# A hybrid decoder layer: a row's product ahead of a copy, exponentials and copies issued with yields between them, and a last norm with a partial sum as bias

## The chip, the cores and the metric

The kernel runs on one core of a Trainium2 chip. The metric is the device time of one execution in microseconds (us); less is better. A core has five engines that work side by side and wait for each other through semaphores: TensorE (in the profile PE, its weight loads PEld), VectorE (DVE), ScalarE (ACT), GpSimd (POOL) and SyncE (SP). DMA queues move data between the chip's memory and the core's SBUF; here SP issues the weight loads, POOL a few large copies. TensorE writes its results to PSUM, which has eight banks; this kernel uses four as accumulators (`acc`) and four for everything else (`aux`).

## The reference, cut to what matters

One decoder layer over 256 tokens of width 2048, with a norm before and a norm after:

```
h = rms_norm(x, pre_norm_w)
proj = h @ w_in                      # one wide projection, split into q/k/v, gates, b, a ...
A: gated delta rule, 8 heads of 128, in chunks of 64
   qkv = silu(causal_conv(gdn_qkv)); q, k unit norm
   g = cumsum(-exp(a_log) * softplus(a + dt_bias))   per chunk
   decay = exp(g_i - g_j) on and below the diagonal
   L = strict lower part of (beta k) k^T * decay
   T = inverse of (L + I);  u = T (beta v);  states carried from chunk to chunk
   oa = rms_norm(o) * gdn_norm_w * silu(z)
B: causal attention, 8 heads of 128 (256 tokens are one block)
   ob = attention(q, k, v) * silu(z)
merged = sigmoid(gate_a) * (oa @ w_branch_a) + sigmoid(gate_b) * (ob @ w_branch_b)
y = merged @ w_out
out = x + rms_norm(y, post_norm_w)
```

All of it is in float32. `decay` needs the exponentials, the inverse of `L + I` needs the triangles, and the last line needs the mean square of each row of `y`: these are the places that the change touches.

## The kernel before

**Products.** TensorE multiplies in a faster format (`F32R`) to nearly full accuracy: each operand is split into `hi` (a cast, on ScalarE, L213) and `lo` (the rest, on VectorE, L214), and a product is made of hi·hi, hi·lo and lo·hi. Weights are loaded 1 MB at a time through SP into one of three `raw` buffers, and split into one of three `hi`/`lo` buffers. A block of projection is either token-major (`proj_n`, L346: two output tiles of 512 columns, 16 steps of six matmuls each) or head-major (`proj_t`, L328: two heads, 8 steps of eight matmuls).

**What runs beside the products.** Every step ends with a call of `tick` (L131). The other work is written as Python generators in queues: `gq` (decay, scores, inverse, solve of branch A), `vq` (its values), `aq` (two queues of attention heads), `mq`. A generator runs up to its next `yield w` and is then left alone for `w` units; a step takes off half a unit. So a `yield 1` puts two steps of the projection between two pieces of work. Nothing is measured while the kernel runs: the yields only fix the order in which instructions are written. `Queue.drain` (L66) runs what is left of a queue with no steps in between.

**How order becomes execution.** `mm` and `tr` (L138, L141), and some operations of other engines, are wrapped in `pin`, which keeps them in program order. TensorE thus executes exactly in program order. Instructions that are not pinned (casts, the DMA issues on POOL, copies) are ordered by a scheduler at build time, which places an instruction on its engine as early as what it needs allows. An engine executes its own list in order, and waits where an instruction's input is not ready.

**The blocks.** `ORDER` (L39) lists the blocks: `q0 mv0 zg0 q1 kq2 kq3 zg1 v0 v1 v2 ga0 zm0 zm1 ga1 mv1 v3 ga2 ga3 mk0 mk1 gb0 mk2 gb1 mk3 gb2 gb3`. Ahead of them stand a first key projection and the block `zg2`, whose last columns feed the decay. A block `kq` is a key and a query block, `mk` a query and a key block of the attention. After the list come the two branch projections (`ua`, `ub`) and the output projection (`y`).

**What the change and the prediction touch.**

- L314 to L325: after the first norm's factor, `rrow` is copied out of PSUM; `prow` (the convolution's weights as rows) is transposed into the tile `pcp` and copied to `pcol`; then a product of one row, `adrow` (the decay's two parameter rows), with ones spreads it over all partitions into other columns of `pcp`, and it is copied to `nad`.
- `decays` (L375): forms the decay's exponents with VectorE, two heads at a time with `yield 1` between, then four exponentials on ScalarE (L441), each over two heads (128x768), in place in `dec`.
- `scores` (L488), one generator a head: splits keys and queries, multiplies, weighs with `dec`.
- `inverse` (L595): once all heads are scored, writes the triangles to `l_d` in memory, copies all of them to the four partition groups of `lc` (L620, four DMAs on POOL of 512 KB each), waits `L_WAIT` (7 units), and then eliminates column by column on VectorE, 63 columns with a yield after each: 0.6 units, or 2 while `after[0]` is positive, which is so for 16 steps after each value block (`SLOW`, L672). Then the inverse goes through `t_d` to `tt`, and another `L_WAIT`.
- `solve` (L692): products with the inverse (`sv`), then for each of the two token tiles `outputs` (L728): products `so` in two groups of four heads, their squares with sums on ScalarE (L744), a factor `fo` (VectorE, a square root on ScalarE, a reciprocal), products with the gate `os` (L760), a yield of `OS_WAIT` (5), transposes `ot`, and a split into `oaT`.
- `attend` (L802): scores `ms`, softmax, transposes `pp`, products `po`, transposes `pt`; the first head to arrive at L838 asks for `ob_tile()`, a tile that lies where `solve` reads its data (`g0`), so `free_tile` (L677) first drains `gq`.
- `weigh` (L1024) and `finish` (L1034): of each 512 columns of `y`, a square with its sum on ScalarE (into one column of `ssy`) and a product with the norm's weights (`yw`, L1031); after the fourth, the sum of the four columns, a square root, a reciprocal, then scaling with the residual added and the store, for one token tile after the other.

Of the kernel before, what the change touches and what calls it, by code (L numbers as in the profile page):

```python
# [8 lines left out]
F32 = mybir.dt.float32  # L9
F32R = mybir.dt.float32r  # L10
BF16 = mybir.dt.bfloat16
AF = mybir.ActivationFunctionType
ALU = mybir.AluOpType
AX = mybir.AxisListType

P = 128
EPS = 1e-6
# [7 lines left out]
D_WAIT = 7  # L25
SC_WAIT = 4
L_WAIT = 7
INV = (0.6, 2)
SLOW = 8
V_WAIT = 8  # L30
# [41 lines left out]
def hybrid_layer(  # L72
# [15 lines left out]
    nc = tc.nc  # L88
    B, S, D = x.shape
    NT = S // P  # L90
    KT = D // P
    H = a_log.shape[1]
# [45 lines left out]
    def mm(*args, **kwargs):  # L138
        return pin(nc.tensor.matmul(*args, **kwargs))  # L139
# [177 lines left out]
    pcol = cst.tile([P, P], F32, name="pcol")  # L317
    pcp = aux_tile("pcp")
    tr(pcp[:, :P], prow, ident)
    nc.vector.tensor_copy(pcol, pcp[:, :P])  # L320

    mm(pcp[:, P : P + nba], ones[0:1, :], adrow, start=True, stop=True)
    nad = cst.tile([P, nba], F32, name="nad")
    nc.vector.tensor_copy(nad, pcp[:, P : P + nba])
    na, dtb = nad[:, :H], nad[:, H:]  # L325
# [49 lines left out]
    def decays():  # L375

        pbt = [pt[:, ZBA:ZW] for pt in pzg]
        zz = cst.tile([P, NT, H], F32, name="zz")
        sp = cst.tile([P, NT, H], F32, name="sp")
        for t in range(NT):  # L380
            pa_ = pbt[t][:, H:]
            pin(nc.vector.scalar_tensor_tensor(zz[:, t, :], pa_, rstd[:, t : t + 1], dtb, op0=ALU.mult, op1=ALU.add))
        for t in range(NT):
            pb_ = pbt[t][:, :H]
            pin(nc.scalar.activation(beta[:, t, :], pb_, AF.Exp, scale=nrstd[:, t : t + 1]))
        pin(nc.scalar.activation(sp, zz, AF.Abs))
        pin(nc.scalar.activation(sp, sp, AF.Exp, scale=-1.0))
        pin(nc.scalar.activation(na, na, AF.Exp))
        pin(nc.scalar.activation(sp, sp, AF.Ln, bias=ones[:, 0:1]))
        pin(nc.vector.scalar_tensor_tensor(sp, zz, 0.0, sp, op0=ALU.max, op1=ALU.add))  # L390
        pin(
            nc.vector.scalar_tensor_tensor(
                sp, sp, -1.0, na.unsqueeze(1).to_broadcast([P, NT, H]), op0=ALU.mult, op1=ALU.mult
            )
        )
        nc.vector.tensor_scalar_add(beta, beta, 1.0)
        nc.vector.reciprocal(beta, beta)
        yield 0.5
        for f in late:
            f()  # L400
        yield PG_WAIT
        pg = aux_tile("pg")
        mm(pg[:, 0:nba], tri_u, sp, start=True, stop=True)
        mm(pg[:, nba : nba + H], ones, sp[:, 0, :], start=True, stop=True)
        nc.vector.tensor_copy(gcol, pg[:, 0:nba].rearrange("p (t h) -> p t h", t=NT))
        nc.vector.tensor_tensor(gx, pg[:, nba : nba + H], gcol[:, 0, :], op=ALU.subtract)
        yield PGT_WAIT
        pgt = aux_tile("pgt")
        tr(pgt[0:nba, :P], gcol.rearrange("p t h -> p (t h)"), ident)
        grs = cst.tile([nba, P], F32, name="grs")  # L410
        nc.vector.tensor_copy(grs, pgt[0:nba, :P])
        g_d = dram.tile([nba, P], F32, name="g_d")
        nc.gpsimd.dma_start(g_d, grs)
        grow = big.tile([P, NT, H, P], F32, tag="z0", name="grow")
        nc.gpsimd.dma_start(
            grow.rearrange("p t h n -> p (t h n)"),
            g_d.rearrange("a n -> (a n)").unsqueeze(0).broadcast_to([P, nba * P]),
        )
        yield D_WAIT
        for h in range(0, H, 2):  # L420
            for h_ in (h, h + 1):
                for t in range(NT):
                    pin(
                        nc.vector.scalar_tensor_tensor(
                            dec[:, h_, 2 * t * P : (2 * t + 1) * P],
                            grow[:, t, h_, :],
                            gcol[:, t, h_ : h_ + 1],
                            mask_t,
                            op0=ALU.subtract,
                            op1=ALU.add,  # L430
                        )
                    )
            nc.vector.tensor_tensor(
                dec[:, h : h + 2, P : 2 * P],
                grow[:, 1, h : h + 2, :],
                gx[:, h : h + 2].unsqueeze(2).to_broadcast([P, 2, P]),
                op=ALU.add,
            )
            yield 1
        for h in range(0, H, 2):  # L440
            pin(nc.scalar.activation(dec[:, h : h + 2, :], dec[:, h : h + 2, :], AF.Exp))  # L441
        decaying.pop()


# [150 lines left out]
    def inverse():  # L595
        lc = big.tile([P, 64, 64], F32, tag="u1", name="lc")
        tv = big.tile([P, 16, 64], F32, tag="tv", name="tv")
        tw = big.tile([P, 16, 64], F32, tag="tw", name="tw")

        nc.gpsimd.memset(tv, 1.0)  # L600
        for g in range(4):
            nc.gpsimd.affine_select(
                out=tv[32 * g : 32 * g + 32],
                in_=tv[32 * g : 32 * g + 32],
                compare_op=ALU.is_equal,
                fill=0.0,
                base=g,
                pattern=[[4, 16], [-1, 64]],
                channel_multiplier=0,
            )  # L610
        for b in range(4):
            t, p_ = b // 2, b % 2
            c0 = t * 4 * P + p_ * 64
            for g in range(2):
                nc.gpsimd.dma_start(
                    l_d[b, g * HG : (g + 1) * HG].rearrange("h j i -> j h i"),
                    gsl[g][p_ * 64 : p_ * 64 + 64, :, c0 : c0 + 64],
                )
        for g in range(4):
            nc.gpsimd.dma_start(  # L620
                lc[32 * g : 32 * g + 32].rearrange("p j i -> p (j i)"), l_d.rearrange("b h j i -> (b h) (j i)")
            )
        yield L_WAIT
        for j in range(63):
            n, r = j // 4 + 1, 63 - j
            pin(
                nc.vector.tensor_tensor(
                    tw[:, :n, :r],
                    lc[:, j : j + 1, j + 1 :].to_broadcast([P, n, r]),
                    tv[:, :n, j : j + 1].to_broadcast([P, n, r]),  # L630
                    op=ALU.mult,
                )
            )
            pin(nc.vector.tensor_tensor(tv[:, :n, j + 1 :], tv[:, :n, j + 1 :], tw[:, :n, :r], op=ALU.subtract))
            yield INV[after[0] > 0]
        for g in range(4):
            nc.gpsimd.dma_start(
                t_d.rearrange("b h (c g) i -> g (b h) c i", g=4)[g], tv[32 * g : 32 * g + 32]
            )
        inv.append(big.tile([P, NT, H, 64], F32, tag="tt", name="tt"))  # L640
        for p_ in range(2):
            for t in range(NT):
                nc.gpsimd.dma_start(
                    inv[0][p_ * 64 : p_ * 64 + 64, t, :, :], t_d[2 * t + p_].rearrange("h c i -> c h i")
                )
        yield L_WAIT

# [376 lines left out]
    def weigh(c, t, pt):  # L1024
        jy = wk.tile([P, 512], BF16, tag="jy", name=f"jy_{c}_{t}")
        cs = slice(c * 512, (c + 1) * 512)
        pin(nc.scalar.activation(jy, pt, AF.Square, accum_out=ssy[t][:, c : c + 1]))
        if c == 3:
            rs = wk.tile([P, 1], F32, tag="rstd", name=f"rs_{t}")
            pin(nc.vector.tensor_reduce(rs, ssy[t], axis=AX.X, op=ALU.add))  # L1030
        pin(nc.vector.tensor_tensor(yw[t][:, cs], pt, postw[:, cs], op=ALU.mult))  # L1031
        return rs if c == 3 else None

    def finish(t, rs):  # L1034
        pin(nc.scalar.activation(rs, rs, AF.Sqrt, bias=epst, scale=1.0 / D))
        pin(nc.vector.reciprocal(rs, rs))
        for i, (c0, c1) in enumerate(((0, 256), (256, 768), (768, 1280), (1280, 1792), (1792, D))):
            cs = slice(c0, c1)
            pin(
                nc.vector.scalar_tensor_tensor(  # L1040
                    yw[t][:, cs], yw[t][:, cs], rs, hx[:, t, cs], op0=ALU.mult, op1=ALU.add
                )
            )
            (nc.sync if i % 2 == 0 else nc.scalar).dma_start(of[t * P : (t + 1) * P, cs], yw[t][:, cs])
# [14 lines left out]
    for kb in range(KT // 4):  # L1059
        raw = wraw.tile([P, 4, 512], F32, tag="raw", name=f"raw_y{c}_{kb}")  # L1060
        nc.sync.dma_start(raw, wo[kb * 512 : (kb + 1) * 512, c * 512 : (c + 1) * 512].rearrange("(k p) c -> p k c", p=P))
        for u in range(2):
# [7 lines left out]
            parts.append((hi, lo))  # L1070
            if i in (1, 3):
                weigh(2, i // 2, pts2[i // 2])
    for t in range(NT):
        for k in range(KT):
            hi, lo = parts[k // 2][0][:, k % 2], parts[k // 2][1][:, k % 2]
# [2 lines left out]
            mm(pts[t], sh, hi, start=(k == 0), stop=False)  # L1078
            mm(pts[t], sh, lo, start=False, stop=False)
            mm(pts[t], sl_, hi, start=False, stop=(k == KT - 1))  # L1080
        finish(t, weigh(c, t, pts[t]))


# [26 lines left out]
```

## Time and profile before

| | |
|---|---|
| time, median of 3 runs | 784.0 us (783.68 to 784.26) |
| the profiled execution's own time | 784.95 us |
| span of its profile, first to last instruction | 783.2 us |
| instructions | 10314 |
| TensorE clock granted, mean | 0.998 |
| memory read, written | 145.42 MB, 3.15 MB |
| rate over the span | 190 GB/s |

The profile is one execution taken by the hardware profiler. Its views name an instruction by source line, engine, operation and tiles, written output<-input, with shapes (partitions x elements). A matmul's duration includes its way through the array, so matmuls overlap and the distance between two starts is what one costs. `[1.13 <-DVE pcol L320]` behind an instruction says that its engine was idle for 1.13 us before it, and what ended that. The view of waits sums these: total us, times, longest. The chain of waits goes back from the last instruction, at each step to what released it. A view by stretches gives each engine's busy time in PE, PEld, DVE, ACT, POOL order with the number of instructions, then the granted clock of TensorE, the DMA engines' busy share and GB/s.

### The profile page before, as it was taken

What the parts mean: (1) busy time and instruction counts of PE and PEld (TensorE: products, weight loads), DVE (VectorE), ACT (ScalarE), POOL (GpSimd) and SP (SyncE); (2) the same over time, 40 slices, a digit from 0 to 9 for tenths busy, and PEclk for the clock granted to TensorE, in tenths of its full rate; (3) what the DMA queues carried; (4) which work ended last, traced back from release to release, by engine and by line L of the source; (5) the groups of instructions that cost most, each with busy time, mean ns of one, the idle gap of its engine ahead of it and who ended that gap; (6) DMA issues with size and microseconds to landing.
All of it is one profiled execution on the core that took longest, in us unless ns stands there. A gap on an engine that the chain in (4) does not pass through costs nothing.

```text
span 783.2 us, 10314 instructions
## 1 busy us (share of the span) xinstructions
PE 770.1 (98%) x3947; PEld 656.7 (84%) x3947; DVE 530.1 (68%) x874; ACT 412.2 (53%) x624; POOL 24.6 (3%) x47
## 2 busy tenths in 40 slices
PE   8999999999999999999999999999999999999995
PEld 7898898898887888888888888888888888888884
DVE  5776669886875998874337566554645668986673
ACT  4667665655564545455355546454464445465551
POOL 3000000010020000011000000000000000000000
PEclk9999999999999999999999999999999999999999
DMA  8566576457587556667435465556556555577542
GB/s 298 172 215 203 163 221 181 153 156 221 190 198 253 199 182 207 199 203 221 130 108 165 159 215 162 170 163 206 162 164 229 198 180 210 191 279 269 163 159 108
DMA packets 92823, 149.24 MB, mean 191 GB/s; under 512 B 3045, under 2 KB 46694, under 8 KB 92134
## 3 DMA queue, kind: packets, MB, share of 16 engines
q1 hardware_dynamic: 89958, 136.51, 54.6%
q0 software_dynamic: 2240, 11.02, 4.8%
q10 hardware_dynamic: 576, 1.05, 0.4%
q8 instruction: 31, 0.51, 0.3%
q14 instruction: 18, 0.15, 0.1%
HBM read 145.42 MB, written 3.15 MB: 190 GB/s over the span
## 4 chain that ended last, share of the span: by engine, by line
PE 91%; DVE 3%; ACT 2%; DMA 2%; issue 1%; SPq 0%; DVEq 0%; ACTq 0%
PE a_gb L139 11%; PE a_y L139 11%; PE a_ga L139 9%; PE a_mq L139 6%; PE a_mk L139 6%; PE a_v L139 6%; PE a_k L139 6%; PE a_zm L139 6%; PE a_mv L139 5%; PE a_ub L139 5%; PE a_zg L139 5%; PE a_ua L139 5%; PE a_q L139 4%; DMA raw_zm<-in_w_in_dram 2%; PE sv L139 2%; PE s L139 1%
## 5 line engine op out<-in xcount | busy, mean ns | idle before, releaser
L139 PE MATMUL a_gb<-hi_gb,hT 128*128 128x512 f32 x256 | 82.4, 395 | 0.0
L139 PE MATMUL a_ga<-hi_ga,hT 128*128 128x512 f32 x256 | 81.7, 393 | 0.0
L214 DVE TENSOR_TENSOR lo_gb<-raw_gb,hi_gb 128x1024 fp32r<-128x1024 f32 x32 | 39.2, 1225 | 41.4 <-ACT hi_gb L213 41.4
L213 ACT CAST hi_gb<-raw_gb 128x1024 fp32r<-128x1024 f32 x32 | 33.6, 1051 | 48.0 <-PE a_gb L139 34.7
L139 PEld LDWEIGHTS a_ga<-hi_ga,hT 128*128 128x128 f32 x256 | 48.1, 188 | 10.6 <-issue 0.7
L139 PEld LDWEIGHTS a_gb<-hi_gb,hT 128*128 128x128 f32 x256 | 48.1, 188 | 10.0
L214 DVE TENSOR_TENSOR lo_ga<-raw_ga,hi_ga 128x1024 fp32r<-128x1024 f32 x32 | 39.1, 1223 | 24.1 <-ACT hi_ga L213 24.0
L213 ACT CAST hi_ga<-raw_ga 128x1024 fp32r<-128x1024 f32 x32 | 33.6, 1052 | 40.1 <-PE a_ga L139 30.8
L139 PE MATMUL a_ga<-lo_ga,hT 128*128 128x512 f32 x128 | 50.0, 390 | 0.0
L139 PE MATMUL a_gb<-lo_gb,hT 128*128 128x512 f32 x128 | 49.8, 389 | 0.0
L139 PE MATMUL a_zg<-hi_zg,hT 128*128 128x348 f32 (+1 forms) x192 | 47.5, 323 | 0.1
L139 PE MATMUL a_mq<-hT,hi_mq 128*128 128x512 f32 x128 | 46.3, 404 | 0.0
L139 PE MATMUL a_mk<-hT,hi_mk 128*128 128x512 f32 x128 | 46.0, 401 | 0.0
L139 PE MATMUL a_y<-hi_y,mT 128*128 128x512 f32 x144 | 45.6, 390 | 0.0
L139 PE MATMUL a_q<-hT,hi_q 128*128 128x512 f32 x128 | 45.4, 397 | 0.0
L139 PE MATMUL a_v<-hT,hi_v 128*128 128x512 f32 x128 | 45.3, 397 | 0.0
L139 PE MATMUL a_ua<-hi_ua,oaT 128*128 128x512 f32 x128 | 41.8, 395 | 0.0
L139 PE MATMUL a_k<-hT,hi_k 128*128 128x512 f32 x128 | 41.3, 406 | 0.0
L139 PE MATMUL a_zm<-hi_zm,hT 128*128 128x512 f32 x128 | 40.7, 393 | 0.0
L139 PE MATMUL a_mv<-hi_mv,hT 128*128 128x512 f32 x128 | 40.1, 391 | 0.0
L139 PE MATMUL a_ub<-hi_ub,obT 128*128 128x512 f32 x128 | 40.1, 389 | 0.0
L139 PE MATMUL a_mq<-hT,lo_mq 128*128 128x256 f32 x128 | 35.9, 281 | 0.0
(317 smaller groups left out, 1909.4 us busy)
## 6 DMA issues: line engine op xcount, KB each, us to landing
raw_ga<-in_w_in_dram SPq DMA_DIRECT2D x16, 1024.0 KB, 5.2
raw_gb<-in_w_in_dram SPq DMA_DIRECT2D x16, 1024.0 KB, 5.1
raw_y<-in_w_out_dram SPq DMA_DIRECT2D x15, 1024.0 KB, 5.3
raw_q<-in_w_in_dram SPq DMA_DIRECT2D x8, 1024.0 KB, 5.7
raw_mv<-in_w_in_dram SPq DMA_DIRECT2D x8, 1024.0 KB, 5.0
raw_v<-in_w_in_dram SPq DMA_DIRECT2D x8, 1024.0 KB, 5.8
raw_zm<-in_w_in_dram SPq DMA_DIRECT2D x8, 1024.0 KB, 5.2
raw_mq<-in_w_in_dram SPq DMA_DIRECT2D x8, 1024.0 KB, 5.8
```

The source lines that it names most:

```text
L139: return pin(nc.tensor.matmul(*args, **kwargs))
L213: nc.scalar.copy(hi, raw)
L214: nc.vector.tensor_tensor(lo, raw, hi.bitcast(F32), op=ALU.subtract)
```

## The change

Four edits, all of them to order and small operations:

1. The product that spreads `adrow` is written ahead of the copy to `pcol`.
2. In `decays`, a `yield 1` stands after each of the first three exponentials.
3. In `inverse`, a yield stands after each of the four copies to `lc` (2, 2, 2 and 4 units) in place of one of 7 after all of them.
4. In the last norm, the sum of the first three columns of `ssy`, scaled and with epsilon added (`so_far`, two small VectorE operations for each token tile), is formed ahead of the last products; the square root takes the fourth column as its input and that sum as its bias. The reduction over four columns between square and root is gone.

```diff
+LC_WAIT = (2, 2, 2, 4)
...
     tr(pcp[:, :P], prow, ident)
+
+    mm(pcp[:, P : P + nba], ones[0:1, :], adrow, start=True, stop=True)
     nc.vector.tensor_copy(pcol, pcp[:, :P])
-
-    mm(pcp[:, P : P + nba], ones[0:1, :], adrow, start=True, stop=True)
     nad = cst.tile([P, nba], F32, name="nad")
...
         for h in range(0, H, 2):
             pin(nc.scalar.activation(dec[:, h : h + 2, :], dec[:, h : h + 2, :], AF.Exp))
+            if h + 2 < H:
+                yield 1
         decaying.pop()
...
             nc.gpsimd.dma_start(
                 lc[32 * g : 32 * g + 32].rearrange("p j i -> p (j i)"), l_d.rearrange("b h j i -> (b h) (j i)")
             )
-        yield L_WAIT
+            yield LC_WAIT[g]
         for j in range(63):
...
         pin(nc.scalar.activation(jy, pt, AF.Square, accum_out=ssy[t][:, c : c + 1]))
-        if c == 3:
-            rs = wk.tile([P, 1], F32, tag="rstd", name=f"rs_{t}")
-            pin(nc.vector.tensor_reduce(rs, ssy[t], axis=AX.X, op=ALU.add))
         pin(nc.vector.tensor_tensor(yw[t][:, cs], pt, postw[:, cs], op=ALU.mult))
-        return rs if c == 3 else None
-
-    def finish(t, rs):
-        pin(nc.scalar.activation(rs, rs, AF.Sqrt, bias=epst, scale=1.0 / D))
+
+    def so_far(t):
+
+        rb = wk.tile([P, 2], F32, tag="mx", name=f"rb_{t}")[:, 0:1]
+        pin(nc.vector.tensor_reduce(rb, ssy[t][:, 0:3], axis=AX.X, op=ALU.add))
+        pin(nc.vector.tensor_scalar(rb, rb, 1.0 / D, EPS, op0=ALU.mult, op1=ALU.add))
+        return rb
+
+    def finish(t, rb):
+        rs = wk.tile([P, 1], F32, tag="rstd", name=f"rs_{t}")
+        pin(nc.scalar.activation(rs, ssy[t][:, 3:4], AF.Sqrt, bias=rb, scale=1.0 / D))
         pin(nc.vector.reciprocal(rs, rs))
...
+    rbs = [so_far(t) for t in range(NT)]
     for t in range(NT):
...
-        finish(t, weigh(c, t, pts[t]))
+        weigh(c, t, pts[t])
+        finish(t, rbs[t])
```

## The prediction

> **What bounds the kernel now.** I read the busy times first, then TensorE's own waits, then the timeline around each of them.
>
> ```profile
> PE 770.1 (98%) x3947; PEld 656.7 (84%) x3947; DVE 530.1 (68%) x874; ACT 412.2 (53%) x624; POOL 24.6 (3%) x47
> ```
>
> ```profile
> PE pcp L139 <- DVE pcol L320: 1.1, 1, 1.1
> ...
> PE a_zm L139 <- DVE lo_zm L214: 0.8, 1, 0.8
> PE a_zg L139 <- DVE lo_zg L214: 0.5, 1, 0.5
> ```
>
> TensorE is busy for 98% of the span; what it waits for between its first product and its last adds up to these three places. So the kernel's time is TensorE's work plus its head, its tail and these gaps. The other engines matter only where they make a gap. Three edits aim at the three gaps and the fourth at the tail; nothing changes the products themselves. The whole prize is therefore small, and a new gap of a few us would cancel it. That is what has to be looked for.
>
> **Edit 1, the row's product ahead of the copy.** Columns of the timeline: start, duration, engine, line, operation.
>
> ```profile
> 35.95 0.27 PE L142 MATMUL pcp<-ident,prow 128*128 128x128 f32 x1
> 36.68 0.42 DVE L316 COPY rrow<-prr 128x256 f32<-128x256 f32 x1
> ...
> 37.35 0.39 PE L139 MATMUL pcp<-adrow,ones 1*128 1x16 f32 x2 [1.13 <-DVE pcol L320]
> 37.67 0.43 PE L139 MATMUL a_zg<-hi_zg,hT 128*128 128x344 f32 x1
> ```
>
> The small product writes other columns of the bank that VectorE is copying from, and sits behind that copy. Moved ahead of it, it follows the transpose at once: the gap of 1.13 goes. The copy now waits for both, but the product ends near 36.6 and VectorE is in the copy of `rrow` until 37.10, so the copy starts no later. Saved: 1.13 (at least nothing, if the projection after it then waits for its split weights).
>
> **Edit 2, the exponentials apart.**
>
> ```profile
> 89.55 1.28 ACT L441 ACT_TABLE_LOAD   x1
> ...
> 90.84 3.05 ACT L441 ACTIVATE dec<-dec 128x768 f32<-128x768 f32 x4
> ...
> 93.51 0.32 PE L139 MATMUL a_zg<-lo_zg,hT 128*128 128x348 f32 x1
> ...
> 94.00 0.32 PE L139 MATMUL a_zg<-lo_zg,hT 128*128 128x348 f32 x1
> ...
> 95.52 0.43 PE L139 MATMUL a_zg<-lo_zg,hT 128*128 128x348 f32 x1 [0.49 <-DVE lo_zg L214]
> ```
>
> The table load and four exponentials hold ScalarE for 4.3 us, and the next cast of weights stands behind them. Products on `lo_zg` come every 0.49 (93.51 to 94.00); this one comes 1.52 later, so 1.03 is lost. With one exponential in every second step, the first costs the casts 1.28 + 0.76 and each later one 0.76, less than the stretch had to spare (4.3 less the 1.03 lost is 3.3). Saved: 1.03. But three yields of one unit, six steps in all (a step is one `tick`, half a unit), now stand ahead of everything in queue `gq`: every score, the inverse and the solve. The scores have no consumer on the path at that point; the inverse and the solve are followed below.
>
> **Edit 3, the copies apart.** The chain of waits gives the first row, the timeline the others.
>
> ```profile
> 225.39 13.68 DMA raw_zm<-in_w_in_dram
> ```
>
> ```profile
> 2.70 0.94 POOL L600 MEMSET tv<- 128x1024 f32 x1
> ...
> 220.77 1.98 POOL L620 DMA_DIRECT2D lc<-l_d  x4 [2.27 <-DMA l_d<-gdn]
> ...
> 240.06 0.39 PE L139 MATMUL a_ga<-hi_ga,hT 128*128 128x512 f32 x1
> ...
> 240.29 0.48 PE L139 MATMUL a_zm<-hi_zm,hT 128*128 128x512 f32 x1
> ...
> 241.53 0.50 PE L139 MATMUL a_zm<-lo_zm,hT 128*128 128x512 f32 x1 [0.76 <-DVE lo_zm L214]
> ...
> 456.80 0.78 POOL L900 DMA_DIRECT2D tq<-in_w_out_dram  x1 [100.11 <-ACT hi_gb L213]
> ```
>
> Four copies (2 MB together) issued in 2 us make a weight load of 1 MB take 13.68. Most of that is covered by loads already in hand: products follow each other in 0.23 (240.06 to 240.29) and the late one comes 1.24 after, so 1.01 is lost. Would the yields keep the copies apart? I think not. A yield only places an instruction later in program order, and GpSimd's stream is not tied to TensorE's steps: it runs what is ready. The memset of `tv`, written beside these copies in `inverse`, ran at 2.70, some 215 us before them; a load written after the last gate block ran at 456.80, in the middle of the gates. So the four still go out back to back when `l_d` has landed, six steps later (36 products of 0.23, 8.3 us) because the scores are later. The burst then starts near 229, after the load that it now delays had been issued at 225.39; it catches the load behind it. The loss is between nothing and the same 1.01 again, and up to about 1 more if it meets a worse moment. I take 0.6 saved: the load behind has more in hand, and the burst is as long.
>
> **Edit 4, the last norm.** The chain of waits at the end, then one row of the timeline.
>
> ```profile
> 775.42 0.70 ACT jy L1027 x2
> ...
> 776.14 0.16 DVE rs L1030
> 776.29 0.60 DVE yw L1031
> 776.89 0.08 DVE rs L1036
> ...
> 777.00 0.48 DVE yw L1040
> ```
>
> ```profile
> 753.70 0.69 DVE L1031 TENSOR_TENSOR yw<-a_y,postw 128x512 f32<-128x512 f32 x1 [1.88 <-ACT jy L1027]
> ```
>
> The chain goes through the product `yw`, not through the square root: the root is beside it. Without the reduction `yw` could start with the square at 775.42, and then the end moves by 0.34 (square 0.70, root about 0.3, a reciprocal, against 777.00). But at 753.70 VectorE sat idle for 1.88 until ScalarE had finished its square on the same tile, so `yw` waits for the square anyway and starts at 776.14 rather than 776.21: 0.07 saved. I take 0.07, nearest to the row; 0.34 is the other end. The four small operations of `so_far` (0.16 each by the reduction) run while TensorE's last products set the time; without that cover they would cost 0.6.
>
> The Trainium skill, PSUM — Partial Sum Buffer, "PSUM bank collisions raise a hardware error", says that two engines may not touch one bank and the same partitions at once, reads included, so that they must be put in sequence. The idle 1.88 agrees; by that rule edit 4 is worth 0.07, without it 0.34.
>
> **What all the yields cost, a new gap.** I count steps from the loop `ORDER`: a token-major block has 16, a head block 8 (`kq` and `mk` 16). Before, the inverse starts at step 135, its first column at 149, it ends at 233 and `solve` issues its first products at 247. The exponentials add 6 (141). The copies' yields add up to 10 units where `L_WAIT` was 7, so 6 more (161). Then more columns fall into the slow stretch of 16 steps after the last value block (step 224), where a column takes 4 steps and not 1.2: columns 53 to 56 rather than the last two. The inverse ends at 248 and `solve` starts at 262, 15 steps late. Its second token tile's output products move from steps 285 and 286 to 300 and 301. At step 301, the 13th of block `gb0`, the first attention head asks for `obT`, whose memory `solve` must have left: `gq.drain()` then issues all that remains, without its waits. Before, all that remained was one group of four transposes whose input was long ready. After, it is the whole second output: squares, factor, two products with the gate, two groups of transposes. TensorE keeps program order, so it stands at the first transposes while the squares and factors are made. The same work before:
>
> ```profile
> 447.20 1.95 PE L139 MATMUL so<-gdn 128*128 128x128 f32 x16
> ...
> 448.90 0.47 PE L139 MATMUL a_mk<-hT,hi_mk 128*128 128x512 f32 x1
> ...
> 449.24 0.28 ACT L744 ACTIVATE jo<-so 128x128 bf16<-128x128 f32 x1 [0.64 <-PE so L139]
> ...
> 450.16 0.22 ACT L744 ACTIVATION_READ_ACCUMULATOR jo<-so 128x1 f32 x1
> ...
> 450.41 0.17 DVE L751 SCALAR_TENSOR_TENSOR fo<-ssoo,fo 128x8 f32<-128x8 f32 x1
> ...
> 451.69 0.21 ACT L754 ACTIVATE fo<-fo 128x8 f32<-128x8 f32 x1
> ...
> 451.93 0.20 DVE L755 RECIPROCAL fo<-fo 128x8 f32<-128x8 f32 x1 [1.35 <-ACT fo L754]
> ...
> 452.24 1.13 DVE L760 SCALAR_TENSOR_TENSOR os<-so,fo,zg 128x128 f32<-128x128 f32 x4
> ```
>
> ```profile
> 472.23 0.60 PE L142 MATMUL ot<-ident,os 128*128 128x128 f32 x4
> ...
> 472.67 0.38 PE L142 MATMUL pt<-ident,om 128*128 128x128 f32 x2
> ```
>
> From TensorE's end of the group (448.90): 0.34 to the first square, 1.14 of squares (to 450.38), 0.2 for the factor, then, with the square root's table still loaded, root to products 0.55 (451.69 to 452.24), products 1.13: 3.4 until the first transposes may start. The second group's products take another 1.13, its transposes 0.44 (472.23 to 472.67): the last ends near 5.0. Without waiting, the head's own transposes (0.22) and the two groups (0.88) take 1.1. So 3.9 is lost. Bounds: 3.4 if the gaps between engines close up, 5.2 if the root needs its 1.28 table load again (in `solve`'s new place the heads' exponentials come ahead of the first root, none behind it, so I take none). Nothing later gives it back: behind the transposes stand `gb0`'s last three steps and everything after, and TensorE has no gap left to absorb it. The inverse's and solve's DMAs keep the 14 steps that they had to land.
>
> Smaller risks from the later place: the first output's products with the gate now share the two buffers `s` with the heads' scores and must wait for their transposes, one step ahead of their own; and scores that hold the buffers of `y` six steps longer let go of two accumulators late. Each 0 to 1.1 (one group of products); together I take 0.4.
>
> **Sum**, against the profiled execution (784.95, of it 783.2 span, 0.95 above the median 784.0): −1.13 − 1.03 − 0.6 − 0.07 + 3.9 + 0.4 = +1.5, 786.4; on the median 785.5. By the bounds of the terms 783.9 to 788.0.
>
> **Rivals.**
>
> Not late enough: the extra steps are taken up somewhere (a queue that runs ahead, a wait replaced and not added), `solve` ends before step 301 and the drain finds its inputs ready. Then only the gains stay: 784.0 − 2.83 = 781.2, 780.5 with 1.01 and 0.34 in full. For it: TensorE loses only these three gaps now, and the drain at step 301 already happens without a gap. Against it: the same count places every step of before where the trace has it (the forced `ot` at 472.23).
>
> The clock falls: TensorE stands for 3.2 (3.4 less the head's 0.22).
>
> ```profile
> 9.00:10.00 1.00, 1.00 (x4) 0.81 (x4) 1.00 (x3) 0.98 (x2) 0.00 (x0) 1.00 1.08 336
> ...
> 13.00:14.00 1.00, 1.00 (x12) 1.00 (x11) 0.00 (x0) 0.26 (x1) 0.00 (x0) 1.00 1.05 399
> ```
>
> ```profile
> 779.00:780.00 1.00, 0.00 (x0) 0.00 (x0) 0.87 (x2) 0.00 (x0) 0.00 (x0) 0.97 0.96 371
> 780.00:781.00 1.00, 0.00 (x0) 0.00 (x0) 0.00 (x0) 0.00 (x0) 0.00 (x0) 0.50 1.02 383
> ```
>
> At the kernel's end the granted clock (third from the right) is 0.50 from about 4.6 after TensorE's last product at 775.3; gaps of 1.13 leave it at full speed. Somewhere between lies the point from which it decides, and 3.2 is between. At the start, matmuls came 4 in a us at 9 to 10 and 12 at 13 to 14; some 3.5 to 5 us at half pace cost 1.7 to 2.5. That gives 787.2 to 788.
>
> The Trainium skill, TensorE: Matmul & The Clock Gate, "What's actually happening", puts the fall at an idle window of about 3.4 us and the return after as much work. By it a gap of 3.2 just passes; a gap with the table load would not, and would cost 1.7 more.
>
> The spread works after all: the copies land apart, the full 1.01 is saved: 785.1. Against it stand the two rows of GpSimd.
>
> **How the numbers follow.** Forecast (slower by the new gap, net) 0.58; clock falls 0.17; not late 0.19; spread works 0.06. About 0.2%, 1.57 us, is what a measurement here can tell from no change: 782.4 to 785.6. The forecast's 785.5 lies at that edge, so half its chance counts as no change (0.29) and half as slower (0.29); the clock adds 0.15 to slower, the spread 0.05 and a little of the clock to no change; the case of not late is faster. Faster 0.20, within 0.2% 0.36, slower 0.44. The range runs from 781.0, which holds most of the case of not late, to 788.0.
>
> **What would show it.** The wait of `pcp` for `pcol` and of `a_zg` for `lo_zg` gone; exponentials of `dec` with casts between them; the four `lc` issues still within 2 us, near 227; a wait of TensorE for `os` of 3 to 5 us in block `gb0`, with `ot` groups right behind `so`; the granted clock after it. It is wrong if no such wait is there, or if `lc`'s issues stand 5 us apart.

## The result, and the profile after

| | before | after |
|---|---|---|
| median of the runs on one chip, us | 783.68 (781.47 to 786.06) | 785.36 (783.84 to 787.10) |
| profiled execution, us | 784.95, span 783.2 | 785.26, span 783.2 |
| ratio | 1 | 1.0023, interval 1.0012 to 1.0034 |

The change costs 1.8 us by the ratio (0.9 to 2.7); 1.5 had been forecast. That both profiled spans are 783.2 is chance: in the profile of after TensorE reaches the small row's transpose 1.00 sooner (34.95 against 35.95), ahead of everything that the change touches; in the three profiles of kernels with the old head it lies anywhere from 34.73 to 35.95. Only distances between rows are therefore compared below.

TensorE's busy time is what it was, from the page's first part, and its waits, from the view of waits, have changed places. The columns of the second are us in total, times, longest.

```profile
PE 770.5 (98%) x3947; PEld 657.4 (84%) x3947; DVE 530.8 (68%) x876; ACT 412.1 (53%) x623; POOL 24.6 (3%) x47
```

```profile
PE ot L143 <- DVE os L763: 2.4, 1, 2.4
PE hTp L143 <- DMA x<-in_x_dram: 1.4, 2, 0.9
PE warm L140 <- DVE epst L174: 1.1, 1, 1.1
```

All three gaps that the change aims at are gone, and one new wait, larger than any of them, stands in the gates. The timeline shows each edit (start, duration, engine, line, operation; line numbers are up to 9 higher than before). First the row's product, then the exponentials:

```profile
34.95 0.27 PE L143 MATMUL pcp<-ident,prow 128*128 128x128 f32 x1
35.15 0.39 PE L140 MATMUL pcp<-adrow,ones 1*128 1x16 f32 x2
35.47 0.42 PE L140 MATMUL a_zg<-hi_zg,hT 128*128 128x344 f32 x1
...
88.64 0.85 ACT L442 ACTIVATE dec<-dec 128x768 f32<-128x768 f32 x1
89.39 0.76 ACT L214 CAST hi_zg<-raw_zg 128x696 fp32r<-128x696 f32 x1
90.06 0.84 ACT L442 ACTIVATE dec<-dec 128x768 f32<-128x768 f32 x1
...
93.23 0.32 PE L140 MATMUL a_zg<-lo_zg,hT 128*128 128x348 f32 x1
93.72 0.32 PE L140 MATMUL a_zg<-lo_zg,hT 128*128 128x348 f32 x1
```

From the transpose to the first projection it is 0.52 (34.95 to 35.47), before 1.72: 1.20 gained. A cast of weights now stands between every two exponentials, and the products on `lo_zg` keep their pace of 0.49 to the end: the 1.03 is gained.

Next the four copies, and the products on `zm` that used to be late behind them; then the end of the last norm.

```profile
226.29 1.98 POOL L623 DMA_DIRECT2D lc<-l_d  x4 [2.30 <-DMA l_d<-gdn]
...
237.09 0.39 PE L140 MATMUL a_zm<-hi_zm,hT 128*128 128x512 f32 x1
237.31 0.39 PE L140 MATMUL a_zm<-lo_zm,hT 128*128 128x512 f32 x1
```

```profile
775.52 0.60 ACT L1030 ACTIVATE jy<-a_y 128x512 bf16<-128x512 f32 x1 [8.52 <-PE a_y L140]
...
776.24 0.69 DVE L1031 TENSOR_TENSOR yw<-a_y,postw 128x512 f32<-128x512 f32 x1 [6.14 <-ACT jy L1030]
...
777.04 1.15 DVE L1047 SCALAR_TENSOR_TENSOR yw<-yw,rs,hx 128x256 f32<-128x256 f32 x2
```

The yields do not part the copies: four issues in 1.98, the same as before. Yet the gap is gone whole (0.22 between the two products, before 1.24). In the norm `yw` still waits for ScalarE's square; from the square to the first scaling it is 1.52, before 1.58 (775.42 to 777.00): 0.06 gained.

And the new wait, in block `gb0`:

```profile
467.20 0.38 PE L143 MATMUL pt<-ident,om 128*128 128x128 f32 x2
467.47 0.28 ACT L747 ACTIVATE jo<-so 128x128 bf16<-128x128 f32 x1 [2.08 <-PE so L140]
...
469.47 2.16 DVE L763 SCALAR_TENSOR_TENSOR os<-so,fo,zg 128x128 f32<-128x128 f32 x8
469.97 2.19 PE L143 MATMUL ot<-ident,os 128*128 128x128 f32 x8 [2.38 <-DVE os L763]
...
471.96 0.63 PE L143 MATMUL pt<-ident,om 128*128 128x128 f32 x2
472.24 0.77 PE L140 MATMUL a_gb<-hi_gb,hT 128*128 128x512 f32 x1
472.81 0.63 PE L140 MATMUL a_gb<-lo_gb,hT 128*128 128x512 f32 x1
473.24 0.96 PE L140 MATMUL a_gb<-hi_gb,hT 128*128 128x512 f32 x2
474.04 0.39 PE L140 MATMUL a_gb<-lo_gb,hT 128*128 128x512 f32 x1
```

The view by stretches of 1 us has PE's busy share after the stretch, and the clock granted to TensorE third from the right:

```profile
470.00:471.00 1.00, 1.00 (x4) 0.56 (x5) 1.00 (x5) 0.00 (x0) 0.00 (x0) 0.78 0.00 0
...
473.00:474.00 1.00, 1.00 (x4) 0.80 (x3) 1.00 (x2) 0.15 (x1) 0.01 (x1) 0.51 0.22 57
474.00:475.00 1.00, 1.00 (x6) 0.78 (x5) 0.00 (x1) 0.30 (x1) 0.00 (x0) 1.00 0.62 164
```

TensorE has the last group of `so` and one head's two transposes behind it at 467.42 (467.20 and twice 0.11) and starts the forced transposes at 469.97. They come one by one, at the pace at which VectorE makes their inputs (2.16 / 8 = 0.27), and are through at 471.96. With their inputs ready, eight transposes at 0.11 would have taken 0.88, so up to here 471.96 − 467.42 − 0.88 = 3.7 are lost. Meanwhile the clock falls to a half: its means of 0.78 and 0.51 in two stretches put the fall near 470.6 and the return near 474.0, 3.4 us, and the products that follow come 0.4 to 0.6 apart and not 0.23. This fall is usual in the changed kernel: the mean granted clock is 0.992 to 0.996 in its thirteen runs, and 0.997 or 0.998 in thirty of the 35 runs of the kernel before that were measured beside four of the experiments below.

### The profile page after: what moved, and what is told of

It reads as the page before. It is cut to its first block, busy times and chain, and to the rows that moved or that the text cites. A ratio compares the mean times of both kernels' runs of the same rounds, so it can differ in the third digit from the quotient of the medians.

```text
span 783.2 us, 10310 instructions
## 1 busy us (share of the span) xinstructions
PE 770.5 (98%) x3947; PEld 657.4 (84%) x3947; DVE 530.8 (68%) x876; ACT 412.1 (53%) x623; POOL 24.6 (3%) x47
## 4 chain that ended last, share of the span: by engine, by line
PE 95%; DVE 2%; ACT 2%; DMA 1%; issue 0%; SPq 0%; DVEq 0%; ACTq 0%
PE a_gb L140 11%; PE a_ga L140 11%; PE a_y L140 11%; PE a_zg L140 6%; PE a_mq L140 6%; PE a_mk L140 6%; PE a_v L140 6%; PE a_k L140 6%; PE a_zm L140 6%; PE a_mv L140 5%; PE a_ub L140 5%; PE a_ua L140 5%; PE a_q L140 4%; PE sv L140 2%; PE s L140 1%; PE so L140 1%
## 5 line engine op out<-in xcount | busy, mean ns | idle before, releaser
L140 PE MATMUL a_v<-hT,lo_v 128*128 128x256 f32 x128 | 35.9, 281 | 0.0
```

## The experiments

Theory: the three gains are real, and the loss is the drain at step 301, which finds the second output unmade because the inverse is 15 steps late; part of that loss is the clock. Rivals: the loss is spread over small waits; the copies' yields do part the transfers; the slow transposes are all clock, or none of it is.

**The inverse early again.** All four edits, only with the copies' yields shorter, so that `solve` ends ahead of step 301.

```diff
-LC_WAIT = (2, 2, 2, 4)
+LC_WAIT = (1, 1, 1, 1)
```

> All four edits, but the copies' yields are 1 unit each: the solve then starts at step 247 as before the change, not at 262. Theory (the only loss is the forced drain of the second output in block gb0, with the fall of the clock behind it): the wait of TensorE for os and the half clock at 470 are gone, the three gaps stay closed, so the time is 3.3 under before: 780.4 on 783.7, ratio 0.9958. Rival (the yields themselves cost, by scores that come later, buffers held longer or a copy burst in a worse place): still near 785, or above before.

Measured: 781.30 against 783.62, ratio 0.9967 (0.9954 to 0.9980), 2.6 us less than before; the lowest median of the study. 3.3 less (0.9958) had been expected, which the interval just includes. TensorE's waits, whole:

```profile
PE hTp L143 <- DMA x<-in_x_dram: 1.6, 2, 1.0
PE warm L140 <- DVE epst L174: 1.1, 1, 1.1
PE a_k L140 <- ACT hi_k L267: 0.2, 1, 0.2
```

The wait for `os` is gone with the lateness, and the gains stay. From the small row's transpose to the last norm's square it is 736.38 (35.16 to 771.54), before 739.47: 3.1 less in this profile. Small losses spread over the kernel can therefore make up some 0.7 by the median, 3.3 less 2.6; they are not the loss of the changed kernel. The rival falls.

**TensorE kept busy through the wait.** Products of ones into the memory of the first forced transposes, ahead of them. They only use time; the transposes overwrite what they leave. First 18 of them, then 10.

```diff
                 pt = aux_tile(f"ot_{t}_{g}")
+                if t == 1 and g == 0:
+                    for _ in range(18):
+                        mm(pt[:, :P], ones, ones, start=True, stop=True)
```

> The changed kernel with 18 extra 128-column products of ones (about 0.11 each at full clock, 2 in all) written into the transposes' own bank just ahead of the first forced transposes, where TensorE stands for 2.4; the real transposes overwrite them. They only keep TensorE busy. Theory (half of the loss at the drain is the granted clock, 3.4 at one half): clock stays at 1, the transposes and first products behind the wait run at full speed, about 1.7 to 2 faster than the changed kernel: 783.5, ratio 0.9997. Rival (the loss is the wait alone and the clock record is a by-product): 785.4 or a little more, ratio 1.002.

Measured: 785.10 against 783.62, ratio 1.0013 (1.0002 to 1.0024). From the timeline:

```profile
467.37 4.18 PE L140 MATMUL ot<-ones 128*128 128x128 f32 x36
471.39 1.04 PE L143 MATMUL ot<-ident,os 128*128 128x128 f32 x8
```

The experiment missed its size: each product is two rows of 0.11, so 18 take 4 us where 2 had been meant, and the transposes start 4.02 behind the head's own two (467.37 to 471.39), in the changed kernel 2.55. The clock stayed at full speed and the eight transposes, their inputs ready, took 0.9 instead of 2.0, so loss and gain are mixed and the time alone, between the two that were expected, says little. Hence the shorter one:

> The changed kernel with 10 small products of ones into the memory of the first forced transposes, ahead of them, in place of 18: about 2.2 us by what 18 took (3.9), so that TensorE stands for about 0.4 and not 2.4, and the transposes start when they did, near 470. If the fall of the clock costs what the slow transposes and first products show (1.1 and 0.9), the clock stays at full speed there and the time is 2.0 us below the changed kernel: 783.3, ratio to the kernel before 0.9996. If those transposes are slow because they follow the products with the gate head by head, the time stays at 785.3, ratio 1.0022.

Measured: 784.41 against 783.69, ratio 1.0006 (0.9993 to 1.0019), that is 0.0016 or 1.25 us under the changed kernel's, though the two intervals overlap (1.0012 there); the rows have to carry the reading. From the timeline, then the stretch in which the clock had fallen before:

```profile
467.70 0.38 PE L143 MATMUL pt<-ident,om 128*128 128x128 f32 x2
467.92 2.40 PE L140 MATMUL ot<-ones 128*128 128x128 f32 x20
469.97 2.16 DVE L763 SCALAR_TENSOR_TENSOR os<-so,fo,zg 128x128 f32<-128x128 f32 x8
470.37 2.14 PE L143 MATMUL ot<-ident,os 128*128 128x128 f32 x8
472.35 0.38 PE L143 MATMUL pt<-ident,om 128*128 128x128 f32 x2
...
473.51 0.39 PE L140 MATMUL a_gb<-lo_gb,hT 128*128 128x512 f32 x1
```

```profile
471.00:472.00 1.00, 0.98 (x5) 0.52 (x5) 1.00 (x5) 0.48 (x1) 0.00 (x0) 1.00 0.00 0
```

At full clock the eight transposes still take 2.0 (470.37 to 472.35): they go at VectorE's pace, so the 1.1 that I had put down to the clock is not the clock's. The two transposes and four products behind them take 1.16 (472.35 to 473.51) and in the changed kernel 2.08 (471.96 to 474.04): this 0.9 is. Over the whole place, from the end of the head's own two transposes ahead of the forced ones, it is 5.59 (467.92 to 473.51) and 6.62 (467.42 to 474.04). Each side of the expectation was right for one half.

**The copies' yields taken out.** Edits 1, 2 and 4 with one wait of 7 units behind the copies.

```diff
-            yield LC_WAIT[g]
+        yield L_WAIT
```

> Edits 1, 2 and 4; the four copies are followed by one wait of 7 as before. By the count of steps the solve starts at 256, its last output group is issued at 295, and the drain at step 301 finds one group of products with the gate still to make: a wait of about 0.7 and no fall of the clock. Theory: gaps closed (3.3), 0.7 lost: 781.1, ratio 0.9967; the copies issue within 2 us at the same place as in the changed kernel and the gap before a_zm is gone although nothing spreads them. Rival (the copies' yields do close that gap): the wait of a_zm for lo_zm is back with about 1.

Measured: 781.90 against 783.62, ratio 0.9975 (0.9963 to 0.9987). Copies and one wait, from the timeline and the view of waits:

```profile
226.39 1.98 POOL L623 DMA_DIRECT2D lc<-l_d  x4 [2.28 <-DMA l_d<-gdn]
```

```profile
PE ms L140 <- DVE y_mk L852: 1.0, 1, 1.0
```

Without edit 3 the gap on `zm` is gone all the same: its yields are not what closed it. The wait of 0.7 that had been expected at the drain is not there. In its place there is a new small wait at 424: the products with the gate of the first output now stand on VectorE ahead of an attention head's keys, `y_mk`, for which that head's scores `ms` wait.

**The exponentials' yields taken out.** Edits 1, 3 and 4.

```diff
-            if h + 2 < H:
-                yield 1
```

> Edits 1, 3 and 4; the exponentials stand together as before. The solve starts at step 256 again, the drain costs about 0.7. The scores are where they were before the change, so the burst of copies is too. Theory (the yields do not spread the copies, the burst was only moved by the exponentials' yields): both the wait of a_zg for lo_zg (1.1 lost) and that of a_zm for lo_zm (about 1) are there; time 783.7 - 1.2 + 0.7 = 783.2, ratio 0.9994. Rival (edit 3 spreads the copies): the wait of a_zm is gone, 782.2.

Measured: 784.04 against 783.62, ratio 1.0000 (0.9987 to 1.0013). Three of TensorE's waits, the copies, and three stretches of 1 us:

```profile
PE a_zm L140 <- ACT hi_zm L214: 1.1, 1, 1.1
PE ms L140 <- DVE y_mk L850: 1.0, 1, 1.0
PE a_zm L140 <- DVE lo_zm L215: 0.8, 1, 0.8
```

```profile
218.31 1.98 POOL L621 DMA_DIRECT2D lc<-l_d  x4 [2.29 <-DMA l_d<-gdn]
```

```profile
239.00:240.00 1.00, 0.50 (x1) 0.19 (x1) 0.97 (x1) 0.98 (x2) 0.00 (x0) 1.00 0.56 205
240.00:241.00 1.00, 0.69 (x3) 0.60 (x4) 1.00 (x2) 1.00 (x1) 0.00 (x0) 1.00 0.13 49
...
242.00:243.00 1.00, 1.00 (x4) 0.82 (x3) 0.42 (x1) 1.00 (x2) 0.00 (x0) 0.50 0.59 113
```

With its own yields in place and the exponentials together, edit 3 parts nothing and closes nothing: the burst goes out at 218 in one piece, and TensorE waits for `zm` 1.9 and not 0.8. That it waits longer is not edit 3's doing: the last run below, without it, shows 2.1. In this execution the clock falls behind the two gaps as well. Of the twelve executions it took longest (786.41), and the fall is by all signs not in every one: the mean granted clock is 0.995 in the three longest and 0.997 or 0.998 in eight of the others.

**Is it the place of the burst?** The kernel before, with everything behind the exponentials six steps later and nothing spread.

```diff
         decaying.pop()
+        yield 3
```

> The kernel before with one yield of 3 behind the last exponential: everything queued behind (scores, copies, inverse, solve) comes six steps later, exponentials and copies both still in one piece. If the place of the burst decides, and not its spread, the four copies go out back to back near 226 to 228, the gap on lo_zm (1.0) is gone, and that on lo_zg (1.0) stays. The inverse is as late as in the kernel without the copies' yields, so the wait of ms for y_mk (1.0 to 1.3) may come: ratio 0.999 without it, 1.000 with it. If it is the exponentials' spread that closed the gap on lo_zm, that gap stays: 1.000 to 1.0015.

Measured: 784.70 against 783.69, ratio 1.0012 (1.0003 to 1.0021), above the 1.000 that was expected with the wait of `ms`, and inside the range of the rival; only the rows tell the two apart.

```profile
229.90 1.99 POOL L621 DMA_DIRECT2D lc<-l_d  x4 [2.27 <-DMA l_d<-gdn]
```

```profile
PE ms L139 <- DVE y_mk L850: 1.0, 1, 1.0
PE a_zg L139 <- DVE lo_zg L214: 0.5, 1, 0.5
```

The exponentials are in one piece (the wait on `lo_zg` is there), the copies too, and the wait on `lo_zm` is gone. It is the place. The wait of `ms` comes with the six steps and costs by its row what the place gained. That leaves the measured 0.9 unexplained; in this profile the distance from the transpose to the last square is longer by 0.4 (739.89 against 739.47).

**Copies really apart.** The kernel before, the copies issued by ScalarE, whose order is tied to the steps.

```diff
+        yield 2
         for g in range(4):
-            nc.gpsimd.dma_start(lc[32 * g : 32 * g + 32]...
-        yield L_WAIT
+            pin(nc.scalar.dma_start(lc[32 * g : 32 * g + 32]...
+            yield (1.5, 1.5, 1.5, 0.5)[g]
```

> The kernel before with the four copies really apart: issued by ScalarE, whose stream is tied to the steps, the first 4 steps later and then 3 steps apart, the inverse at its old step. If four copies at once are what delays the weight load, the issues stand about 4 us apart, the load of zm takes less than its 13.7 us, the gap on lo_zm (1.0) goes, and the time is 1.0 us below: ratio 0.9987. If it is the 2 MB that matter and not that they come at once, a gap of the same size stays there or comes a block later: 1.000. If the inverse's first columns now wait for the last copy, VectorE stands and TensorE with it: over 1.001.

Measured: 784.54 against 783.69, ratio 1.0007 (0.9997 to 1.0017): no gain. First and last issue, and the waits:

```profile
218.65 0.35 ACTq L622 DMA_DIRECT2D lc<-l_d  x1
...
225.47 0.33 ACTq L622 DMA_DIRECT2D lc<-l_d  x1
```

```profile
PE a_ga L139 <- DVE lo_ga L214: 1.3, 2, 0.8
PE a_ga L139 <- ACT hi_ga L213: 0.2, 1, 0.2
```

Over 6.8 us and not 2, the same 2 MB delay the block ahead, `ga`, by more than they delayed `zm`. Spread this far they only choose another load to delay. The run changes two things beside the spread: the copies leave through ScalarE's queue and not GpSimd's, and the first is not later, as was meant, but 0.9 sooner when counted from the small row's transpose (183.9 against 184.8). What each of these does was not separated, and whether the copies would be harmless when spread further was not tried.

**The first and the last edit alone.** No new yield.

```diff
+    mm(pcp[:, P : P + nba], ones[0:1, :], adrow, start=True, stop=True)
     nc.vector.tensor_copy(pcol, pcp[:, :P])
...
+        finish(t, rbs[t])
```

> The row's product ahead of its copy and the last norm's bias alone, without any new yield. If the two are worth what the traces of the full change show (1.2 us in front of the first projection's second product, 0.1 at the end), the time is 1.3 us below the kernel before, ratio 0.998, the gaps of TensorE on lo_zg (about 1.0) and lo_zm (about 1.0) stay as before, the solve stays early, so that there is no wait for os and no fall of the clock in the gates. The rival, that the gap in the head is hidden by the weights that arrive later, gives a ratio of 1.000.

Measured: 782.68 against 783.69, ratio 0.9988 (0.9977 to 0.9999), 0.9 less. The gap on `lo_zg` is there as before. The one on `zm` is larger:

```profile
PE a_zm L140 <- ACT hi_zm L214: 1.3, 1, 1.3
PE a_zm L140 <- DVE lo_zm L215: 0.8, 1, 0.8
```

In this profile TensorE comes to `zm` sooner by what edit 1 gained and by an earlier head, and the load there is no sooner by as much; behind the two gaps the clock is at 0.50 from 240.0 to 243.4. The profiled execution is the second longest of the twelve (784.77). So where the burst keeps its old place, part of a gain in the head can be given back at `zm`; how much of it in the median run, this does not tell.

## Why the prediction came out as it did

The forecast of 785.5 met the measured 785.36, and the reason given for it, gains of about 3 and a new gap of about 4 at step 301, is what the traces show. Not every term was right. That the sum comes so close is luck: the clock's 0.9, which its sum left out, stands against 0.4 of edit 3, 0.4 of risks and 0.2 of the drain.

- **Edit 1**, −1.13: the distance between rows shrank by 1.20. Right.
- **Edit 2**, −1.03: right, and with the whole 1.03. Its other effect, the burst moved, was in the text of edit 3.
- **Edit 3**, −0.6: that the yields do not part the copies was right, and the runs without them and with real distances bear it out. That the loss would come back at the load behind was wrong: the burst in its later place delays nothing that TensorE waits for. −1.01 was the size, the bound that I had named but not taken. The gain is edit 2's, whose six steps move the burst, not edit 3's.
- **Edit 4**, −0.07: 0.06 by the rows. The product `yw` still waits for the square on its tile: it starts at 776.24, 0.72 after the square (775.52), though it needs no more of TensorE than the square does. The Trainium skill, PSUM — Partial Sum Buffer, "PSUM bank collisions raise a hardware error", has two engines on one bank put in sequence; the trace agrees with its 0.72.
- **The drain at step 301**, +3.9: place, cause and size right, its inner course not. I let the first transposes wait for a whole group of products with the gate and so had TensorE stand for 3.2. In fact each transpose follows its own product: TensorE stands for 2.4, less than the 3 to 5 that was to show it, and the transposes then crawl at 0.27. The end is the same, 3.7 lost up to the last of them, since VectorE's eight products (2.16) set it either way.
- **The clock falls**, a rival with 0.17, did come on top: 0.9, not 1.7 to 2.5, because the first half of the slow stretch lies under transposes that wait for VectorE anyway. Forecast and rival were not exclusive, as the chances had them. The length of 3.5 to 5 us was read off two stretches that hold products of different widths (512 columns at 9 to 10, mostly transposes of 128 at 13 to 14) and show the full clock in both, so they did not give it; measured are 3.4.
- **Smaller risks**, +0.4: none in the changed kernel. In three other kernels the outputs moved to another place and met `ms` instead, for 1.0: a risk of this kind is real but all or nothing.

By the rows −1.20 − 1.03 − 1.01 − 0.06 + 3.7 + 0.9 = +1.3, inside the ratio's 0.9 to 2.7. What remains of 1.8 is not told apart from noise. In the two profiles the whole distance from the small row's transpose to the last norm's square grew by 1.1 (739.47 to 740.57), where the terms without edit 4 make 1.4, so by rows too some 0.3 stays open. The range's upper end, 788.0, had edit 1 at its full gain and no further loss from edit 3, though their texts allowed worse; it was not tested by this result.

**Not late enough** was the rival that the run with shorter yields made true: 0.9967 of 784.0 is 781.4, where 781.2 had been worked out for it. That figure had edit 3 at 0.6; by the gap of 1.01 that did close it would have been 780.8, so this closeness too is in part luck. **Spread works** is refuted by the copies' own rows, within 1.98 of each other with the yields as without; the copies from ScalarE add that this much real spread did not pay either.

## What to carry to other kernels

A yield in a hand-written order is paid for by everything behind it in the same queue: count on to the last item, and look for a point that forces the queue empty, since there the lateness, free until then, is paid at once. A yield moves a DMA issue only if something ahead on its engine, or its data, is tied to the steps; otherwise the transfer goes out when its data are ready, whatever the text says. And when an edit's gain shows, try it without the edit: here the copies' gap was closed by the exponentials' yields.

## What was not expected of the hardware

The granted clock fell after less idle time than I had allowed for. In the changed kernel it fell to 0.50 after a wait of 2.4, with nothing but transposes next to it. In the kernel without the exponentials' yields it fell at 241.4 after two waits of 1.1 and 0.8, with products between and behind them: TensorE was busy for 0.50 and 0.69 of the two us from 239 to 241, and for 1.57 of the 3.41 ahead of the fall. The first and last edit alone show the same after 1.3 and 0.8 (1.41 busy of 3.41), and the fastest kernel's profile has the clock at 0.50 in the head, from 7.4 to 10.9, after 0.6 and 1.0. A single gap of 1.1, as before the change, brought no fall in these profiles, and by the mean granted clock the pair of gaps did so in some executions of one kernel and not in others.

The Trainium skill, TensorE: Matmul & The Clock Gate, "What's actually happening", puts the fall at one idle window of about 3.4 us, in windows that run freely. The slow stretch of 3.4 us agrees with such a window, and windows that run freely would let the same gaps count in one execution and not in the next; that a window has to be idle throughout does not agree with the runs that have products between their gaps, and the measurement decides. How much of a window must be idle they leave open, and so does the changed kernel's own trace whether transposes keep the clock up as products do.
